# A low part made by an adding DMA instead of VectorE, for every second weight tile of the S5 input projection

## The chip, the cores and the metric

One core of a Trainium2 chip runs the whole kernel. The metric is the device time of one execution in microseconds (us). Before the change it was run three times: 1904.86, 1898.52 and 1904.84 us, a median of 1904.84 us. One further execution was profiled. Engines are named as the profile names them: PE is TensorE's matmul side and PEld its weight loads, DVE is VectorE, ACT is ScalarE, POOL is GpSimd, SP is SyncE, which here only issues DMAs.

## The reference, cut to what matters

The network has two layers over 256 frames of width 2048, a gated linear attention layer and an S5 layer, each with an inner width of 4096. The change lies in the first product of the S5 layer:

```python
proj = u_in @ w_in                 # (256, 2048) @ (2048, 8192), float32
u, z = jnp.split(proj, 2, axis=-1)
...                                # u drives the recurrence, z becomes silu(z)
```

## The kernel before

All weights are float32 and come from HBM in tiles of 128 partitions x 1024 (two blocks of 128 rows by 512 columns, 512 KB). To multiply in the faster fp32r format without losing accuracy, each weight is written as a sum of two fp32r numbers: `hi`, the weight rounded by ScalarE (line 109), and `lo`, the weight minus `hi`, made by VectorE (line 110). The activations are split in the same way, and a product takes three matmuls: hi x hi (line 155), hi x lo of the activation (line 156) and lo of the weight x hi (line 157). The helper `split` makes the two parts, `wload` issues the load on SP's queue, and `st_step` the 24 matmuls of a tile.

The S5 input projection runs in two loops of 64 tiles each: `su` (the half that becomes u, line 1020) and `sz` (the half that becomes z, line 1099). Each is 8 column groups `g` of 8 tiles `kp`. Between the tiles, other work of the layer is worked off: in `su` the preparation of the S5 kernels (`b_pow`, `b_tr`, `s_mm`, `k_out`; the last writes a block `ks` to the DRAM tensor `dk` by a DMA on POOL's queue, line 986) and the recurrence (`scan`); in `sz` the rest of the recurrence and, for each of 32 blocks `f`, `cload` and `mload` (DMAs `cl<-rec` and `mt<-dk` on SP's queue), `cunit` (VectorE products `wc` from `cl`, lines 912 and 913), `xstage` (a VectorE transpose `xT`, line 1066, then a TensorE transpose `psxs`, line 1069) and `ystage` (matmuls `psy`, and a gelu). After `sz` the product with the gate weights (`gl`) begins.

What sets the order: each engine works through its own instructions strictly in the order that a scheduler fixed when the program was built, and waits at each for semaphores. Buffers rotate: `hi` and `lo` have three buffers each, the loaded weight tile `w` has four in this stage, `cl` and `mt` two each. So ScalarE's rounding of tile n+3 must wait until TensorE has done with tile n, and the load of tile n+4 until both readers of tile n's `w` are done (after the change the planned reuse of these four buffers is at a few places three or five tiles on).

Of the kernel before, what the change touches and what calls it, by code (L numbers as in the profile page):

```python
# [8 lines left out]
F32 = mybir.dt.float32  # L9
F32R = mybir.dt.float32r  # L10
AF = mybir.ActivationFunctionType
ALU = mybir.AluOpType
# [3 lines left out]
P = 128  # L16
D = 2048
E = 4096
# [15 lines left out]
def trunk(ctx, tc, x, c, ln_g, ln_b, ada_w, ada_b, gla_w_in, gla_gate_w2, gla_gate_b, gla_norm_g,  # L34
# [3 lines left out]
    V, S, PE = nc.vector, nc.scalar, nc.tensor  # L38
    dma = nc.sync.dma_start
    wdma = nc.gpsimd.dma_start  # L40

    def pool(name, bufs=1, **kw):
        return ctx.enter_context(tc.tile_pool(name=name, bufs=bufs, **kw))
# [3 lines left out]
    hp = pool("whi", 3)  # L47
    lp = pool("wlo", 3)
# [26 lines left out]
    def psm(name):  # L75
        return mm.tile([P, 512], F32, tag="mm", name=name)
# [19 lines left out]
    def pump(rate=1.0):  # L96
        pace[0] += rate
        while pace[0] >= 1.0:
            pace[0] -= 1.0
            if bg:  # L100
                bg.pop(0)()


    last_lo = [None]

    def split(w, name):
        hi = hp.tile([P, 1024], F32R, tag="hi", name="hi" + name)
        lo = lp.tile([P, 1024], F32R, tag="lo", name="lo" + name)
        S.copy(hi, w)  # L109
        last_lo[0] = V.tensor_tensor(lo, w, hi.bitcast(F32), op=ALU.subtract).ins  # L110
        return hi.rearrange("p (k c) -> p k c", k=2), lo.rearrange("p (k c) -> p k c", k=2)
# [15 lines left out]
    def wload(src, k0, c0, name):  # L127
        ring.append(ring.pop(0))
        w = ring[-1]("w" + name)
        dma(w.rearrange("p (k c) -> p k c", k=2),  # L130
            src[k0 * P:(k0 + 2) * P, c0:c0 + 512].rearrange("(k p) c -> p k c", p=P))
        return w
# [13 lines left out]
    def st_step(banks, u, w, kp, last, first=0):  # L146

        hi, lo = w
        for f in range(4):
            for kk in range(2):  # L150
                k = 2 * kp + kk
                wh = hi[:, kk, f * P:(f + 1) * P]
                wl = lo[:, kk, f * P:(f + 1) * P]
                o = banks[f][:, :T]
                PE.matmul(o, lhsT=wh, rhs=u.hi(k), start=(k == first), stop=False)  # L155
                PE.matmul(o, lhsT=wh, rhs=u.lo(k), start=False, stop=False)  # L156
                PE.matmul(o, lhsT=wl, rhs=u.hi(k), start=False, stop=(k == last))  # L157
# [621 lines left out]
    for g in range(8):  # L779
# [3 lines left out]
        for kp in range(8):  # L783
            for _ in range(-(-len(hq) // (8 * (2 - g % 2) - kp))):
                hq.pop(0)()
            w = split(wload(win, 2 * kp, 6144 + g * 512, f"z{g}{kp}"), f"z{g}{kp}")
# [101 lines left out]
    sw = s5_w_in[0]  # L888
# [53 lines left out]
    def s_in(f, ps):  # L942
        v = tp.tile([P, 2, 16, 8], F32, tag="vv", name=f"vv{f}", bufs=2)
        V.transpose(v.rearrange("p b i s -> p s b i"), ps[:, :T].rearrange("p (s b i) -> p s b i", s=8, b=2)[:, ::-1])
        pu = psx(f"psu{f}")
        for b in range(2):
            PE.transpose(pu[:, b * P:(b + 1) * P], v[:, b].rearrange("p i s -> p (i s)"), ident)
        U = Ut[f // 8][:, f % 8]
        S.copy(U, pu[:, :T].rearrange("p (b r) -> p b r", b=2))
# [50 lines left out]
    def bstep(n):  # L1000
        for _ in range(n):
            if bq:
                bq.pop(0)()

    def scan(cidx, h):
        X = sx[:, h, cidx].rearrange("p (r k) n -> p r k n", r=2)
        N = sx[:, h, cidx + 1].rearrange("p (r k) n -> p r k n", r=2)
        t1 = tp.tile([P, 2, 2, 32], F32, tag="sc1", name=f"sca{cidx}{h}", bufs=1)
        t2 = tp.tile([P, 2, 2, 32], F32, tag="sc2", name=f"scb{cidx}{h}", bufs=1)
        lr = l8r.rearrange("p (k n) -> p k n", k=2)[:, :, 32 * h:32 * h + 32]  # L1010
        li = l8i.rearrange("p r (k n) -> p r k n", k=2)[:, :, :, 32 * h:32 * h + 32]
        V.tensor_tensor(t1, X, lr.unsqueeze(1).to_broadcast([P, 2, 2, 32]), op=ALU.mult)
        V.tensor_tensor(t2, X[:, ::-1], li, op=ALU.mult)
        V.tensor_tensor(t1, t1, t2, op=ALU.add)
        V.tensor_tensor(N, N, t1, op=ALU.add)

    for g in range(8):
        banks = [psm(f"su{g}{f}") for f in range(4)]
        for kp in range(8):
            w = split(wload(sw, 2 * kp, g * 512, f"su{g}{kp}"), f"su{g}{kp}")  # L1020
            st_step(banks, u1, w, kp, 15)
            if (g, kp) == (1, 0):
                b_pace[0] = -1.0
            b_pace[0] += 1.5 if g else 0.25
            n = max(0, int(b_pace[0]))
            bstep(n)
            b_pace[0] -= n
            pump(SCAN_RATE)
        for i in range(4):
            s_in(4 * g + i, banks[i])  # L1030
        if g == 4:
            bg.extend([lambda cidx=cidx: scan(cidx, 0) for cidx in range(1, 31)])
# [30 lines left out]
    def xstage(f):  # L1063
        xt_ = tp.tile([P, 2, 4, 32], F32, tag="xt", name=f"xT{f}", bufs=1)
        n = 2 * (f % 16)
        V.transpose(xt_, sx[:, f // 16, 0:32, :, n:n + 2].rearrange("p c r b -> p b r c"))
        px = psx(f"psxs{f}")
        for b in range(2):
            PE.transpose(px[:, b * P:(b + 1) * P], xt_[:, b].rearrange("p r l -> p (r l)"), ident)
        xs = tp.tile([P, 2, 128], F32, tag="xs", name=f"xS{f}", bufs=2)  # L1070
        S.copy(xs, px[:, :T].rearrange("p (b r) -> p b r", b=2))
        xss[f] = xs

    def ystage(f):
        xs = xss[f]
        py = psx(f"psy{f}")
        U = Ut[f // 8][:, f % 8]
        for b in range(2):
            o = py[:, b * P:(b + 1) * P]
            for q in range(4):  # L1080
                PE.matmul(o[32 * q:32 * q + 32], lhsT=U[:, b, 32 * q:32 * q + 32], rhs=mt[f][:, :, 2 * q + b, :], start=True, stop=False)
            for w in wc[f]:
                for q in range(4):
                    PE.matmul(o[32 * q:32 * q + 32], lhsT=xs[:, b, 32 * q:32 * q + 32],
                              rhs=w[:, 2 * q + b].rearrange("p n i -> p (n i)"), start=False, stop=(w is wc[f][-1]))
        yt = tp.tile([P, 8, 32], F32, tag="yt", name=f"yt{f}", bufs=2)
        V.transpose(yt, py[:, :T].rearrange("p (b t i) -> p t b i", b=2, t=8))
        S.activation(U, yt.rearrange("p t c -> p (t c)").rearrange("p (b r) -> p b r", b=2), AF.Gelu_apprx_tanh)

    def cside(f):  # L1090
        cload(f)
        mload(f)
        cunit(f)

    zs = [s8t(f"zs{i}", [8, T]) for i in range(4)]
    for g in range(8):
        banks = [psm(f"sz{g}{f}") for f in range(4)]
        for kp in range(8):
            w = split(wload(sw, 2 * kp, E + g * 512, f"sz{g}{kp}"), f"sz{g}{kp}")
            st_step(banks, u1, w, kp, 15)  # L1100
            if g == 0:
                bstep(1 + kp % 2)
            pump(SCAN_RATE if g == 0 else Y_RATE)
        for f in range(4):
            i = (g * 4 + f) % 8
            S.activation(zs[g // 2][:, i, :], banks[f][:, :T], AF.Silu)  # L1106
        if g == 0:
            bstep(len(bq))
            while bg:
                bg.pop(0)()  # L1110
            tp.close()
            tp.open("tmp2")
            sc1 = [lambda cidx=cidx: scan(cidx, 1) for cidx in range(1, 31)]
            for f in range(34):
                for _ in range(3):
                    if sc1:
                        bg.append(sc1.pop(0))
                if f < 32:
                    bg.append(lambda f=f: cside(f))
                if 1 <= f < 33:  # L1120
                    bg.append(lambda f=f: xstage(f - 1))
                if f >= 2:
                    bg.append(lambda f=f: ystage(f - 2))
# [18 lines left out]
    for g in range(8):  # L1142
        banks = [psm(f"gl{g}{f}") for f in range(4)]
        for kp in range(16):
            w = split(wload(s5_w_glu[0], 2 * kp, g * 512, f"gl{g}{kp}"), f"gl{g}{kp}")
# [121 lines left out]
```

## Time and profile before

| what | value |
|---|---|
| runs | median 1904.84 us (1898.52 to 1904.86) |
| the profiled execution, own time | 1901.91 us |
| its span, first to last instruction | 1900.0 us, granted TensorE clock 0.987 |
| `su`: first to last matmul with `lo` | 783.4 to 1057.9 us, 64 tiles |
| `sz`: the same | 1058.3 to 1330.1 us, 64 tiles |
| matmuls of line 155 in `su` / in `sz` | 512 / 512 |

A row of a group view gives the line of the kernel, the engine, the operation, output and inputs by the program's names, how often, the busy time in us and the mean of one in ns, then the engine's idle time just before these instructions and what ended it. Matmuls are pipelined: one of 0.28 us starts every 0.12 us. A row of a view of waits gives who waited for whom, the total in us, how often, and the longest. A row of a windows view gives a stretch of the span, the busy us of each engine, the granted clock, the mean busy share of the 16 DMA engines and the rate they moved. A row of a timeline gives start, duration, engine, line and operation, and in brackets the engine's idle time before it and what ended that.

### The profile page before, as it was taken

How to read it: one execution, taken by the hardware profiler on the slowest of the kernel's cores; microseconds unless marked ns; L12 is line 12 of the kernel's file. 1: busy time of each engine (PE TensorE's matmuls, PEld its weight loads, DVE VectorE, ACT ScalarE, POOL GpSimd, SP SyncE). 2: the span in 40 equal slices, each digit the busy share in tenths (PEclk: the TensorE clock that was granted, in tenths of full speed). 3: DMA queues.
4: the chain of work that ended last, by engine and by line, in shares of the span. 5: the costliest groups of instructions: out<-in, count | busy, mean ns of one | idle time of the engine just before them, and what ended most of it. 6: DMA issues, size and time to landing. Idle time of an engine off the chain costs nothing.

```text
span 1900.0 us, 35655 instructions
## 1 busy us (share of the span) xinstructions
PE 1833.9 (97%) x14479; PEld 1649.2 (87%) x14479; DVE 1431.4 (75%) x1992; ACT 890.8 (47%) x1229; POOL 27.0 (1%) x44
## 2 busy tenths in 40 slices
PE   7999999999999999899999989999999999999997
PEld 3787797799999888789899889888999999998886
DVE  2788676889899887687799789988577674457555
ACT  3533365655555333654454445445444444444332
POOL 0000000000000000000000000000000000000000
PEclk9999999999999999899999999999999999999998
DMA  9878975789889997555555577897688886558662
GB/s 358 309 254 275 337 245 183 243 281 321 289 286 310 360 339 242 174 153 153 162 143 159 157 207 218 222 244 216 214 270 256 264 265 205 180 184 322 195 194 68
DMA packets 239501, 449.27 MB, mean 236 GB/s; under 512 B 19220, under 2 KB 45262, under 8 KB 238054
## 3 DMA queue, kind: packets, MB, share of 16 engines
q1 hardware_dynamic: 235400, 437.53, 72.3%
q0 software_dynamic: 3168, 8.41, 1.4%
q8 instruction: 114, 1.87, 0.4%
q10 hardware_dynamic: 768, 1.05, 0.2%
q14 instruction: 51, 0.42, 0.1%
HBM read 432.49 MB, written 14.42 MB: 235 GB/s over the span
## 4 chain that ended last, share of the span: by engine, by line
PE 64%; issue 9%; DVE 7%; DMA 5%; ACT 1%; POOL 1%; SPq 0%; DVEq 0%; POOLq 0%; ACTq 0%
PE gl L157 7%; PE gl L155 7%; PE gl L156 6%; PE op L143 6%; PE op L144 6%; PE op L142 6%; PE z L157 3%; PE z L155 3%; PE z L156 3%; DMA cl<-rec 3%; PE su L155 2%; PE su L157 2%; PE su L156 2%; PE sz L155 1%; PE sz L157 1%
## 5 line engine op out<-in xcount | busy, mean ns | idle before, releaser
L155 PE MATMUL gl<-yh,higl 128*128 128x256 f32 x1024 | 291.9, 285 | 3.3 <-ACT higl L109 3.3
L157 PE MATMUL gl<-yh,logl 128*128 128x256 f32 x1024 | 290.1, 284 | 0.0
L156 PE MATMUL gl<-yl,higl 128*128 128x256 f32 x1024 | 290.1, 283 | 0.0
L110 DVE TENSOR_TENSOR logl<-wgl,higl 128x1024 fp32r<-128x1024 f32 x128 | 156.7, 1225 | 139.0 <-ACT higl L109 138.9
L109 ACT CAST higl<-wgl 128x1024 fp32r<-128x1024 f32 x128 | 134.0, 1047 | 202.7 <-PE gl L156 201.0
L155 PEld LDWEIGHTS gl<-yh,higl 128*128 128x128 f32 x1024 | 197.2, 193 | 4.4 <-ACT higl L109 3.5
L156 PEld LDWEIGHTS gl<-yl,higl 128*128 128x128 f32 x1024 | 197.2, 193 | 1.0 <-issue 1.0
L157 PEld LDWEIGHTS gl<-yh,logl 128*128 128x128 f32 x1024 | 197.1, 193 | 0.2 <-DVE logl L110 0.2
L109 ACT CAST hio<-wo 128x1024 fp32r<-128x1024 f32 x105 | 110.7, 1054 | 173.0 <-PE op L144 159.6
L110 DVE TENSOR_TENSOR loo<-wo,hio 128x1024 fp32r<-128x1024 f32 x105 | 128.4, 1224 | 78.3 <-ACT hio L109 77.8
L242 DVE SCALAR_TENSOR_TENSOR acc<-wa,cs,acc 128x512 f32<-128x512 f32 x215 | 160.8, 748 | 4.1 <-DMA wa<-in_ada_w 1.3
L157 PE MATMUL sz<-u1h,losz 128*128 128x256 f32 x512 | 147.1, 288 | 5.2 <-DVE losz L110 5.2
L155 PE MATMUL sz<-u1h,hisz 128*128 128x256 f32 x512 | 150.7, 295 | 0.2 <-ACT zs L1106 0.2
L155 PE MATMUL su<-u1h,hisu 128*128 128x256 f32 x512 | 150.3, 295 | 0.0
L155 PE MATMUL z<-u0h,hiz 128*128 128x256 f32 x512 | 148.7, 290 | 0.5 <-ACT hiz L109 0.5
L156 PE MATMUL su<-u1l,hisu 128*128 128x256 f32 x512 | 147.1, 288 | 0.0
L157 PE MATMUL su<-u1h,losu 128*128 128x256 f32 x512 | 147.0, 288 | 0.0
L157 PE MATMUL z<-u0h,loz 128*128 128x256 f32 x512 | 145.1, 283 | 1.7 <-DVE loz L110 1.7
L156 PE MATMUL sz<-u1l,hisz 128*128 128x256 f32 x512 | 146.1, 285 | 0.0
L156 PE MATMUL z<-u0l,hiz 128*128 128x256 f32 x512 | 144.7, 283 | 0.0
L142 PE MATMUL v<-hiv,u0h 128*128 128x512 f32 x256 | 103.9, 413 | 4.5 <-ACT hiv L109 2.6
L143 PE MATMUL v<-lov,u0h 128*128 128x512 f32 x256 | 103.5, 405 | 4.4 <-DVE lov L110 4.3
(318 smaller groups left out, 4714.5 us busy)
## 6 DMA issues: line engine op xcount, KB each, us to landing
wgl<-in_s_w_glu SPq DMA_DIRECT2D x128, 512.0 KB
wa<-in_ada_w SPq DMA_DIRECT2D x115, 512.0 KB
a<-in_ada_w SPq DMA_DIRECT2D x32, 1024.0 KB
wv<-in_gla_w_in SPq DMA_DIRECT2D x64, 512.0 KB
wz<-in_gla_w_in SPq DMA_DIRECT2D x64, 512.0 KB
wsu<-in_s_w_in SPq DMA_DIRECT2D x64, 512.0 KB
wsz<-in_s_w_in SPq DMA_DIRECT2D x64, 512.0 KB
wo<-in_s_w_out SPq DMA_DIRECT2D x64, 512.0 KB
```

The costliest lines, as they stand in the source:

```text
L109: S.copy(hi, w)
L110: last_lo[0] = V.tensor_tensor(lo, w, hi.bitcast(F32), op=ALU.subtract).ins
L142: PE.matmul(banks[tt], lhsT=uh, rhs=hi[:, kk, :], start=(k == first), stop=False)
L143: PE.matmul(banks[tt], lhsT=uh, rhs=lo[:, kk, :], start=False, stop=False)
L144: PE.matmul(banks[tt], lhsT=ul, rhs=hi[:, kk, :], start=False, stop=(k == last))
L155: PE.matmul(o, lhsT=wh, rhs=u.hi(k), start=(k == first), stop=False)
L156: PE.matmul(o, lhsT=wh, rhs=u.lo(k), start=False, stop=False)
L157: PE.matmul(o, lhsT=wl, rhs=u.hi(k), start=False, stop=(k == last))
L242: V.scalar_tensor_tensor(acc[0], w[:, kk, :], cs[:, k:k + 1], acc[0], op0=ALU.mult, op1=ALU.add)
```

## The change

For odd `kp` in both loops a new helper is used. ScalarE writes `hi` as before, and then writes minus `hi` into `lo`; after that an accumulating DMA on POOL's queue adds the loaded weight tile, SBUF to SBUF, onto `lo`. VectorE's subtraction goes away for these 64 tiles. Even `kp` stays as it was.

```diff
+    def split_dma(w, name):
+
+        hi = hp.tile([P, 1024], F32R, tag="hi", name="hi" + name)
+        lo = lp.tile([P, 1024], F32R, tag="lo", name="lo" + name)
+        S.copy(hi, w)
+        S.mul(lo, hi.bitcast(F32), -1.0)
+        wdma(lo, w, accum_op=ALU.add)
+        return hi.rearrange("p (k c) -> p k c", k=2), lo.rearrange("p (k c) -> p k c", k=2)
...
-            w = split(wload(sw, 2 * kp, g * 512, f"su{g}{kp}"), f"su{g}{kp}")
+            w = (split_dma if kp % 2 else split)(wload(sw, 2 * kp, g * 512, f"su{g}{kp}"), f"su{g}{kp}")
...
-            w = split(wload(sw, 2 * kp, E + g * 512, f"sz{g}{kp}"), f"sz{g}{kp}")
+            w = (split_dma if kp % 2 else split)(wload(sw, 2 * kp, E + g * 512, f"sz{g}{kp}"), f"sz{g}{kp}")
```

All lines below the helper stand nine lower in the changed file (line 986 is 995, 1039 is 1048). In names such as `losu23` the digits are g and kp.

On POOL's queue, in the middle of `su`, before the change only the writes of `ks` stand:

```order
L986 DMA dk_183<-ks3_8400 8x16x128 [waits DMASW1_49,DVE_49]
L986 DMA dk_183<-ks4_8508 8x16x128 [waits DMASW2_49,DVE_49]
L986 DMA dk_183<-ks5_8620 8x16x128 [waits DMASW3_49,DVE_49]
L986 DMA dk_183<-ks6_8728 8x16x128 [waits DMASW4_49,DVE_49]
L986 DMA dk_183<-ks7_8868 8x16x128 [waits DMASW5_49,DVE_49]
```

The same place on POOL's queue after the change:

```order
L112 DMA losu23_8468<-wsu23_8465 128x1024 [waits DMAHW6_49,DMASW4_49,Activation_49]
L995 DMA dk_183<-ks3_8409 8x16x128 [waits DVE_49]
L112 DMA losu25_8577<-wsu25_8574 128x1024 [waits DMAHW3_49,DMASW6_49,Activation_49]
L995 DMA dk_183<-ks4_8518 8x16x128 [waits DMASW5_49,DVE_49]
L112 DMA losu27_8690<-wsu27_8687 128x1024 [waits DMAHW5_49,DMASW0_49,Activation_49]
L995 DMA dk_183<-ks5_8631 8x16x128 [waits DMASW7_49,DVE_49]
```

Each adding DMA now stands between two writes of `ks`, so that it starts only after the write ahead of it, which waits for VectorE, has been issued.

On ScalarE's queue in `su`, the rounding of two tiles before the change:

```order
L109 CAST hisu30_8764<-wsu30_8762 128x1024
L939 COPY wbt8_8604<-pswb80_8605 128x512
L939 COPY wbt8_8604<-pswb81_8611 128x512
L979 COPY ks5_8620<-psk5_8617 128x128
L109 CAST hisu31_8814<-wsu31_8812 128x1024
L969 COPY kT7_8674<-pss7_8656 128x256
```

And two tiles after the change:

```order
L118 CAST hisu24_8526<-wsu24_8524 128x1024
L948 COPY wbt6_8393<-pswb60_8394 128x512
L948 COPY wbt6_8393<-pswb61_8400 128x512
L988 COPY ks3_8409<-psk3_8406 128x128
L110 CAST hisu25_8576<-wsu25_8574 128x1024
L111 ACTIVATE losu25_8577<-hisu25_8576 128x1024
L978 COPY kT5_8463<-pss5_8445 128x256
```

The row of line 111 is new, straight behind the rounding of the odd tile; the copies keep their places among the roundings, and `kT` and all that follows stands one instruction later. An even tile has no second instruction.

On SP's queue early in `sz`, before the change, with what each load waits for:

```order
L130 DMA wsz21_12172<-in_s5_w_in 128x2x512 [waits DMAHW1_49,DVE_49]
L130 DMA wsz22_12214<-in_s5_w_in 128x2x512 [waits DMAHW2_49,DVE_49]
L130 DMA wsz23_12267<-in_s5_w_in 128x2x512 [waits DMAHW4_49,DMAHW3_49,DVE_49]
L1058 DMA mt2_11970<-dk_183 128x1x1024 [waits PE_49]
L130 DMA wsz24_12331<-in_s5_w_in 128x2x512 [waits DMAHW5_49,DMAHW0_49,DVE_49]
L130 DMA wsz25_12373<-in_s5_w_in 128x2x512 [waits DMAHW6_49,DMAHW1_49,DVE_49]
L1039 DMA cl4_12250<-rec_182 128x256 [waits DMAHW7_49,DVE_49]
```

And after the change:

```order
L139 DMA wsz21_12212<-in_s5_w_in 128x2x512 [waits DMAHW1_49,DMASW4_49,Activation_49]
L139 DMA wsz22_12255<-in_s5_w_in 128x2x512 [waits DMAHW2_49,DVE_49]
L1067 DMA mt2_12009<-dk_183 128x1x1024 [waits DMAHW3_49,PE_49]
L139 DMA wsz23_12308<-in_s5_w_in 128x2x512 [waits DMAHW4_49,DMAHW0_49,DVE_49]
L1048 DMA cl4_12291<-rec_182 128x256 [waits DMAHW5_49,DVE_49]
L1050 DMA cl4_12291<-rec_182 64x128 [waits DMAHW6_49]
L139 DMA wsz24_12373<-in_s5_w_in 128x2x512 [waits DMASW5_49]
```

A load that takes over the buffer of an odd tile (here those of tiles 21 and 24) now waits for the semaphore of a POOL DMA (DMASW) where it waited for VectorE (DVE), and the loads of `mt` and `cl` stand one to two places earlier among the weight loads.

## Prediction

> **What bounds the kernel now.** I read the page first, then windows over the two loops, then the waits inside them.
>
> ```profile
> PE 1833.9 (97%) x14479; PEld 1649.2 (87%) x14479; DVE 1431.4 (75%) x1992; ACT 890.8 (47%) x1229; POOL 27.0 (1%) x44
> ```
> ```profile
> 880.00:920.00 40.00, 39.34 (x405) 35.77 (x405) 32.20 (x42) 20.10 (x38) 2.39 (x4) 1.00 0.56 163
> 1000.00:1040.00 40.00, 39.71 (x428) 35.59 (x426) 39.87 (x95) 19.16 (x35) 2.98 (x5) 1.00 0.54 154
> 1160.00:1200.00 40.00, 39.52 (x465) 37.52 (x464) 39.17 (x77) 18.77 (x28) 0.00 (x0) 1.00 0.88 238
> 1240.00:1280.00 40.00, 36.28 (x474) 33.78 (x474) 35.52 (x39) 18.41 (x28) 0.00 (x0) 0.96 0.92 238
> ```
>
> The columns are PE, PEld, DVE, ACT and POOL, then the clock, the DMA share and GB/s. TensorE is the bound. In `su` (the first two rows) it is busy for over 39 of 40 us even where VectorE is full (39.87), so relieving VectorE has nothing to give there. In `sz` VectorE is nearly full and TensorE loses a few us per 40; that is all that can be won. The DMA engines are at 0.54 to 0.56 in `su`, but at 0.88 and 0.92 in `sz`. The waits within `sz`:
>
> ```profile
> PE psxs L1069 <- DVE xT L1066: 9.4, 3, 3.7
> DVE wc L913 <- DMA cl<-rec: 9.1, 6, 2.5
> ACT hisz L109 <- DMA wsz<-in_s_w_in: 13.6, 3, 7.1
> PE sz L157 <- DVE losz L110: 5.2, 2, 5.0
> ```
>
> TensorE waited directly for the subtraction only twice, 5.2 us. Its 9.4 us for `xT` are VectorE's too, but VectorE itself had been waiting for the `cl` loads (9.1 us): the more so as the DMAs are slow.
>
> **What is removed and added.**
>
> ```profile
> L110 DVE TENSOR_TENSOR losu<-wsu,hisu 128x1024 fp32r<-128x1024 f32 x64 | 77.5, 1211 | 12.4 <-ACT hisu L109 12.0
> L109 ACT CAST hisu<-wsu 128x1024 fp32r<-128x1024 f32 x64 | 67.2, 1050 | 77.3 <-issue 36.8 <-PE su L156 34.3 <-PE op L144 5.0
> ```
>
> 64 subtractions of 1.21 us leave VectorE, 77 us in all. ScalarE gets 64 more instructions over the same 128x1024; I price one at its cast, 1.05 us, 67 us in all. ScalarE is busy 20 of 40 us and stays under two thirds; in `su` it idles after most casts (the timeline below), so I cost this at nothing. Without that cover, each would delay the copies behind it by 1.05 us. The adding DMA is the unknown, as no DMA of before adds or goes from SBUF to SBUF. The nearest rows are POOL's own DMAs, from issue to landing: 64 KB of `ks` (first pair) and 1 MB into `rec` (second pair).
>
> ```profile
> L986 POOL DMA_DIRECT2D dk<-ks x32: 597/597/630, 832.6 to 1098.1; - x32
> DMA to landing us min/median/max: 2.0/3.5/4.4
> ...
> L516 POOL DMA_DIRECT2D rec<-lc x2: 1175/1252/1328, 260.3 to 265.1; - x2
> DMA to landing us min/median/max: 6.8/8.0/10.9
> ```
>
> 512 KB on the straight line between the medians is 3.5 + 4.5 x 448/960 = 5.6 us. An adding DMA must also fetch the bytes it adds onto, which makes it 1 MB read and 512 KB written, so 8.0 would be the full doubling. I take **6.3 us**, nearer to the lower since start and writing do not double. The ends are 2.0 and 10.9 us.
>
> In the Trainium skill, "Collectives: The Full Stack", section "The bandwidth ceiling: the fold count and why AG ≠ RS ≠ AR", an add inside a DMA costs no time of its own, but its two source reads share one read queue and halve the rate. No run here shows that yet; by it the landing is nearer to 8.0 us and the sum below comes to about 1954 us, as an estimate (half of 1.7 us on 28 tiles of `su` most of all).
>
> **When must it land?** With three buffers, the cast of a tile starts as TensorE ends the tile three before. TensorE then needs this tile's `lo` after two tiles, that is, about when the cast two places on starts. From this interval the cast and the new instruction go off, 2.1 us; the rest is the DMA's. ScalarE's timeline in the middle of `su`, at the start of `su`, and at two places of `sz`:
>
> ```profile
> 896.17 1.05 ACT L109 CAST hisu<-wsu 128x1024 fp32r<-128x1024 f32 x1 [1.57 <-PE su L156]
> ...
> 900.65 1.06 ACT L109 CAST hisu<-wsu 128x1024 fp32r<-128x1024 f32 x1 [1.62 <-issue]
> ...
> 904.58 1.05 ACT L109 CAST hisu<-wsu 128x1024 fp32r<-128x1024 f32 x1 [1.69 <-PE su L156]
> ```
> ```profile
> 796.18 1.05 ACT L109 CAST hisu<-wsu 128x1024 fp32r<-128x1024 f32 x1
> ...
> 801.02 1.05 ACT L109 CAST hisu<-wsu 128x1024 fp32r<-128x1024 f32 x1 [1.31 <-PE su L156]
> ...
> 806.78 1.05 ACT L109 CAST hisu<-wsu 128x1024 fp32r<-128x1024 f32 x1 [1.46 <-PE su L156]
> ```
> ```profile
> 1090.34 1.05 ACT L109 CAST hisz<-wsz 128x1024 fp32r<-128x1024 f32 x1 [1.94 <-PE sz L156]
> ...
> 1093.59 1.21 ACT L1106 ACTIVATE zs<-sz 128x256 f32<-128x256 f32 x4
> 1094.66 1.07 ACT L109 CAST hisz<-wsz 128x1024 fp32r<-128x1024 f32 x1
> ...
> 1097.42 1.05 ACT L109 CAST hisz<-wsz 128x1024 fp32r<-128x1024 f32 x1
> ...
> 1102.28 1.05 ACT L109 CAST hisz<-wsz 128x1024 fp32r<-128x1024 f32 x1 [1.83 <-PE sz L156]
> ```
> ```profile
> 1128.23 1.03 ACT L109 CAST hisz<-wsz 128x1024 fp32r<-128x1024 f32 x1
> ...
> 1135.81 1.05 ACT L109 CAST hisz<-wsz 128x1024 fp32r<-128x1024 f32 x1 [1.12 <-DMA cl<-rec]
> ```
>
> Middle of `su`: 8.41 - 2.1 = 6.3 us. The DMA just fits: **0**. A stall would count half, since a stall of one odd tile lies inside the interval of the next.
>
> Start of `su` (tiles 5 and 7, counted from its first cast), while tiles still follow closely: 4.84 - 2.1 = 2.7 us for tile 5, so 3.6 us late; tile 7 has 5.76 - 2.1 = 3.7, which the stall of tile 5 lengthens past 6.3. **+3.6**.
>
> Second column group of `sz`: the cast behind the four `zs` copies waits for the end of the first group, so it is the third tile (kp 2) and those at 1090.34, 1097.42 and 1102.28 are odd. The first has 7.1 - 2.1 = 5.0 and is 1.3 late; the next 4.9 - 2.1 + 1.3 = 4.1, 2.2 late. **+3.5**. The third was one of the two that waited for VectorE, 5.0 us; landing 2.1 + 6.3 us after its cast, it waits about half as long: **-2.7**.
>
> From 1120 to 1190:
>
> ```profile
> 1120.00:1160.00 40.00, 23.67 (x85) 16.07 (x84) 12.09 (x10) 1.00 0.74 217
> 1160.00:1190.00 30.00, 20.04 (x71) 13.39 (x70) 12.21 (x10) 1.00 0.82 229
> 1190.00:1330.00 140.00, 68.49 (x240) 46.34 (x240) 33.26 (x28) 0.98 0.87 228
> ```
>
> These rows count the matmuls on `losz` alone, eight to a tile: 156 in the first two, so some 10 odd tiles. Each has 7.58 - 2.1 = 5.5, is 0.8 late, and counts half: **+4**.
>
> The rest of `sz` (third row) has fewer matmuls per us, so the landing fits. But its DMAs are at 0.87 with 228 GB/s. If that share is real work, full is 228/0.87 = 262 GB/s. 240 matmuls are 30 tiles, 15 of them odd; 15 adding DMAs of 0.5 to 1 MB bring 56 to 112 GB/s more, 284 to 340. Over 262 that would stretch 140 us by 12 to 42 us. Against it, the page shows 360 GB/s in a slice of another stage:
>
> ```profile
> GB/s 358 309 254 275 337 245 183 243 281 321 289 286 310 360 339 242 174 153 153 162 143 159 157 207 218 222 244 216 214 270 256 264 265 205 180 184 322 195 194 68
> ```
>
> At that rate nothing would stretch. I take **+12**, the lower of the two stretches and also 2 us on each of the six `cl` waits above; bounds 0 and 42. Late weight buffers go into it: an odd tile's buffer comes free only with the landing, SP waits for that in order, and the loads of `cl` and `mt` stand behind it; the 13.6 us above show that weight loads are late at times already.
>
> VectorE's relief: the 9.4 us for `xT` partly go, since a subtraction or two stands ahead of them, though the `cl` load ends last: **-5**, bounds 0 and -9.4.
>
> On POOL, an adding DMA stands behind a write of `ks`. Two of these in the middle of `su`:
>
> ```profile
> 895.21 0.60 POOL L986 DMA_DIRECT2D dk<-ks  x1 [8.40 <-DVE ks L983]
> 904.45 0.60 POOL L986 DMA_DIRECT2D dk<-ks  x1 [8.65 <-DVE ks L983]
> ```
>
> The one at 895.21 is past before the cast at 896.17 and its second instruction end (898.3): 0. If VectorE made `ks` 3 us later, POOL would hold up the adding DMA.
>
> The sum: 3.6 + 3.5 - 2.7 + 4 + 12 - 5 = +15.4. The profiled execution took 1901.91 us itself (span 1900.0), 2.9 below the median of the runs, so **1917 us**, 0.6% above the median.
>
> **The rivals.** (1) *Everything lands in time*, and the queues swallow the rest. For it: 5.6 us on the straight line, 360 GB/s elsewhere. Then no stall is added, and VectorE's relief stands: -5.2 for the two waits and up to -9.4, so 1887 to 1902. This is the case that ends on the other side; it decides at 2.7 us at the few close tiles and 5.5 us elsewhere in `sz`. (2) *The adding DMA is far slower*, at the 10.9 us end: (10.9 - 6.3)/2 for 28 tiles of `su` is +64, (10.9 - 5.5)/2 for 32 of `sz` +86, with the 12 above some 2060 us. Against it: 10.9 was 1 MB written to DRAM. (3) *The DMA engines become the bound* of the last 140 us: +42 in place of +12, 1947 us. (4) *VectorE's relief changes nothing*, being no bound, and the new costs are as small: within 0.5% of the median.
>
> A rule that speaks against the change: the Trainium skill, "SBUF — State Buffer", section "Who interferes with whom", says that POOL's building of descriptors is held up while VectorE works in a mode with two ports. In this trace the 32 issues above took 597 to 630 ns beside a full VectorE, so nothing of it shows.
>
> **How the numbers follow.** A measurement tells about 0.5% from no change, 1895 to 1914 us. The forecast with rival 3 (1914 to 1965): 0.40. Rival 4 and the upper part of rival 1 (1895 to 1914): 0.33. The lower part of rival 1 (1885 to 1895): 0.17. Rival 2: 0.10. So slower 0.50, same 0.33, faster 0.17. The range 1888 to 1965 leaves out rival 2 and the lowest part of rival 1, some 0.17.
>
> **What would show it.** The landing of the adding DMAs: about 6 us right, under 5 rival 1, over 9 rival 2. TensorE's waits for a DMA into `lo`: a few us early in `su`, most in `sz` before 1190. The DMA share after 1190: near 1.00 for the forecast and rival 3, and longer waits for `cl`. VectorE's busy time should fall by 77 us, ScalarE's rise by 67. The prediction is wrong if TensorE never waits for `lo`, or if it waits all through `su`.

## The result, and the profile after

The changed kernel takes 1970.4 us (1968.72 to 1971.91, 4 runs) against 1904.31 us (1898.52 to 1904.86): a ratio of 1.035, 95% interval 1.0331 to 1.0369. The profiled execution took 1968.72 us, its span is 1967.0 us. The prediction was 1917 us, slower as it came out, but its range ended at 1965.

First the page: busy time of the engines, then the POOL queue's packets, MB and share of the time of the 16 DMA engines (1.4% before).

```profile
PE 1859.2 (95%) x14479; PEld 1669.4 (85%) x14479; DVE 1375.4 (70%) x1928; ACT 956.6 (49%) x1293; POOL 83.9 (4%) x108
...
q0 software_dynamic: 12384, 41.97, 10.4%
```

VectorE has 64 instructions less and 56 us of busy time less, not the 77 us forecast: the 1.21 us of a row overlap its neighbours at both ends (897.38 + 1.21 is past the next start, 898.51, and the one before it ran to 897.54). ScalarE has 64 more and 66 us more. The same four stretches as before, in the windows view of the changed kernel (the two of `sz` lie some 20 us earlier in its work, as `su` ends later):

```profile
880.00:920.00 40.00, 38.06 (x395) 34.10 (x388) 26.47 (x34) 22.26 (x38) 6.17 (x9) 1.00 0.79 214
1000.00:1040.00 40.00, 37.80 (x401) 33.77 (x398) 36.38 (x89) 23.91 (x40) 6.66 (x9) 1.00 0.76 205
1160.00:1200.00 40.00, 32.21 (x336) 30.39 (x335) 29.34 (x65) 18.39 (x25) 3.37 (x4) 0.87 0.89 227
1240.00:1280.00 40.00, 31.78 (x376) 29.68 (x378) 24.52 (x28) 19.62 (x29) 2.92 (x4) 0.87 0.96 238
```

The next to last column is the DMA share. In `su` it rose from about 0.55 to 0.78 and TensorE, full before, now loses about 2 us in 40. In `sz` it stands at 0.89 and 0.96, and TensorE loses 8. The same view over each whole loop, from its first to its last matmul, first of the kernel before, then of the changed one:

```profile
782.10:1058.20 276.10, 273.16 (x2798) 249.44 (x2797) 235.69 (x401) 142.13 (x263) 15.58 (x26) 0.99 0.55 160
1058.00:1330.40 272.40, 255.89 (x3118) 239.29 (x3116) 237.55 (x359) 131.82 (x207) 3.58 (x6) 0.98 0.78 212
```
```profile
782.40:1078.00 295.60, 278.69 (x2798) 252.93 (x2797) 208.63 (x369) 174.98 (x295) 44.89 (x58) 0.98 0.78 207
1077.80:1396.80 319.00, 275.50 (x3118) 256.07 (x3116) 211.70 (x331) 164.96 (x241) 30.23 (x37) 0.92 0.91 232
```

The second column is the length: `su` grew from 276.1 to 295.6 us, `sz` from 272.4 to 319.0. That is the whole loss, 66 us; the rest of the kernel after `sz` takes 570 us in both. Length times share is the time of the DMA engines: 152 us before and 231 after in `su`, 212 and 290 in `sz`, 78 to 79 us more in each.

The loss in `sz` has two parts. Length minus the busy time of PE grew from 16.5 to 43.5 us, and the same 3118 matmuls were busy for 19.6 us longer (275.50 against 255.89). The clock column fits the second part: 0.02 of 272.4 us and 0.08 of 319.0 us are 5 and 26 us of full-speed time. Over the runs below, the clock of a loop tends to be lower where TensorE stood idle longer: in `su` 0.99 with 2.9 us idle (before), 0.98 with 16.9 (after), 0.94 with 27.8 (e6), 0.86 with 96 (e3). So some 20 of the 46.6 us seem to come on top of the waits. No run holds the clock fixed, so it is not shown that the waits lower it. The other engines did not slow down: a cast took 1.05 us and a `wc` product 1.22 us (medians) in both kernels.

By column group (last `lo` matmul of a group to that of the next, us):

| groups | before | after | difference |
|---|---|---|---|
| `su` 1 | 27.7 | 34.7 | +7.0 |
| `su` 2 to 8 | 246.8 | 259.4 | +12.6 |
| `sz` 1 | 35.0 | 34.4 | -0.6 |
| `sz` 2 | 31.8 | 37.3 | +5.5 |
| `sz` 3 and 4 | 57.5 | 73.6 | +16.1 |
| `sz` 5 to 8 | 147.5 | 173.2 | +25.7 |

The two parts of `sz` differ. The windows of groups 2 to 4 and of groups 5 to 8, before and after:

```profile
1093.20:1182.60 89.40, 83.99 (x900) 80.72 (x899) 80.70 (x163) 41.88 (x60) 1.12 (x2) 0.98 0.75 212
1182.60:1330.10 147.50, 137.46 (x1859) 127.68 (x1857) 133.55 (x165) 72.67 (x118) 0.00 (x0) 0.98 0.86 228
```
```profile
1112.40:1223.30 110.90, 92.06 (x900) 87.56 (x899) 77.30 (x171) 53.68 (x72) 10.87 (x13) 0.91 0.89 230
1223.30:1396.50 173.20, 148.61 (x1858) 137.52 (x1857) 116.29 (x132) 90.84 (x138) 13.46 (x16) 0.91 0.96 240
```

In groups 5 to 8 the DMA engines work for 166 us (0.96 of 173.2), more than the 147.5 us that these groups took before.

The changed kernel's view of the tile `losu`, then of `losz`: the new ScalarE instruction, POOL's issue, and the landing (the first three figures of an instruction's row are ns, least, median, most).

```profile
L111 ACT ACTIVATE losu<-hisu x32: 1057/1058/1087, 772.3 to 1064.9; 128x1024 fp32r<-128x1024 f32 x32
L112 POOL DMA_DIRECT2D losu<-wsu x32: 828/865/917, 773.6 to 1066.2; - x32
...
  PE su L166: 5.6, 4
...
DMA to landing us min/median/max: 4.5/5.9/8.4
```
```profile
  PE sz L166: 40.2, 16
...
DMA to landing us min/median/max: 4.5/6.6/10.8
```

So the adding DMA landed as fast as assumed (6.3 us), and in `su` TensorE waited for a low part only 5.6 us in all, in `sz` 40.2. The waits of the changed kernel in `sz` that answer to those shown of before:

```profile
PE sz L166 <- DMA losz<-wsz: 40.2, 16, 5.2
...
DVE wc L922 <- DMA cl<-rec: 15.6, 8, 4.3
...
DVE wc L921 <- DMA cl<-rec: 6.5, 3, 4.8
```

Read alone, this says that `sz` lost 40 us to late low parts (18.8 in groups 2 to 4, 21.5 in groups 5 to 8) and `su` some 14 us to something else. The experiments bear that out for groups 2 to 4 in the main. In groups 5 to 8 that wait is where the loss shows, not what makes it.

### The profile page after: what moved, and what is told of

It is laid out like the page before. It is cut to its first block, busy times and chain, and to the rows that moved or that the text cites. A ratio compares the mean times of both kernels' runs of the same rounds, so it can differ in the third digit from the quotient of the medians.

```text
span 1967.0 us, 35864 instructions
## 1 busy us (share of the span) xinstructions
PE 1859.2 (95%) x14479; PEld 1669.4 (85%) x14479; DVE 1375.4 (70%) x1928; ACT 956.6 (49%) x1293; POOL 83.9 (4%) x108
## 3 DMA queue, kind: packets, MB, share of 16 engines
q10 hardware_dynamic: 768, 1.05, 0.2%
## 4 chain that ended last, share of the span: by engine, by line
PE 66%; DMA 10%; DVE 4%; issue 4%; ACT 2%; SPq 1%; DVEq 0%; POOLq 0%; POOL 0%; ACTq 0%
PE gl L164 6%; PE gl L165 6%; PE gl L166 6%; PE op L151 6%; PE op L152 6%; PE op L153 6%; DMA losz<-wsz 4%; PE z L166 3%; PE z L164 3%; PE z L165 3%; PE su L164 2%; DMA rb<-rec 2%; PE su L166 2%; PE su L165 2%; PE sz L166 2%
## 5 line engine op out<-in xcount | busy, mean ns | idle before, releaser
L118 ACT CAST hio<-wo 128x1024 fp32r<-128x1024 f32 x105 | 110.9, 1056 | 172.9 <-PE op L153 158.5
L166 PE MATMUL sz<-u1h,losz 128*128 128x256 f32 x512 | 155.7, 307 | 40.4 <-DMA losz<-wsz 40.2
L164 PE MATMUL sz<-u1h,hisz 128*128 128x256 f32 x512 | 157.8, 309 | 0.0
L165 PE MATMUL sz<-u1l,hisz 128*128 128x256 f32 x512 | 153.1, 300 | 0.0
L166 PEld LDWEIGHTS sz<-u1h,losz 128*128 128x128 f32 x512 | 107.0, 210 | 45.0 <-DMA losz<-wsz 43.8
L164 PEld LDWEIGHTS sz<-u1h,hisz 128*128 128x128 f32 x512 | 106.5, 208 | 6.7 <-issue 6.0
```

## The experiments

Landing theory: TensorE loses the time by waiting for low parts that come too late for three buffers. Load theory: the adding DMAs take time of the 16 DMA engines, other loads land later, and TensorE loses it whether or not it waits for a low part. In the diffs below, `-` and `+` are against the changed kernel unless it is said otherwise; line numbers shift by a few where lines were added. Lengths of `su` and `sz` are from the first to the last matmul of the loop. The kernel before was run beside each set; its medians were 1902.7 to 1904.3 us, and the ratios go by these. Lengths come from one profiled execution of each run; where two runs have the same code in a loop, their lengths there differ by 3.6 us at most (`sz` of after and e1).

| run | what | time, us | ratio to before, 95% | `su` | `sz` |
|---|---|---|---|---|---|
| before | | 1904.3 | | 276.0 | 272.4 |
| after | | 1970.4 | 1.0331 to 1.0369 | 295.6 | 319.0 |
| e1 | only `sz` changed | 1954.7 | 1.0248 to 1.0301 | 276.3 | 322.6 |
| e2 | only `su` changed | 1924.5 | 1.0088 to 1.0120 | 295.6 | 271.8 |
| e3 | chained dummies | 2023.4 | 1.0606 to 1.0647 | 400.6 | 271.7 |
| e4 | no low part on odd tiles | 1902.3 | 0.9976 to 1.0001 | 276.4 | 273.8 |
| e5 | 48 dummies from `lo` | 1959.0 | 1.0281 to 1.0314 | 310.5 | 293.2 |
| e6 | four buffers | 1979.3 | 1.0375 to 1.0429 | 314.8 | 312.7 |
| e7 | ScalarE's part alone | 1902.1 | 0.9979 to 1.0004 | 275.6 | 272.2 |
| e8 | plain copy | 1944.8 | 1.0204 to 1.0241 | 284.3 | 302.4 |
| e9 | half of `rb` and `mt` | 1938.6 | 1.0167 to 1.0197 | 284.2 | 302.2 |
| e10 | e9's control, from before | 1886.2 | 0.9892 to 0.9921 | 273.6 | 259.8 |
| e11 | half of the adding DMAs | 1944.8 | 1.0173 to 1.0227 | 285.2 | 305.3 |
| e12 | e9 with four buffers | 1929.9 | 1.0099 to 1.0167 | 282.4 | 292.0 |
| e13 | e6 with six weight buffers | 1975.3 | 1.0335 to 1.0431 | 304.4 | 307.8 |
| e14 | e13 with half of `rb` and `mt` | 1935.1 | 1.0127 to 1.0193 | 279.7 | 288.6 |
| e15 | 64 dummies onto `w` | 1982.7 | 1.0369 to 1.0451 | 314.8 | 312.2 |
| e16 | e12 and half of `cl` | 1916.3 | 1.0055 to 1.0099 | 284.8 | 278.2 |
| e17 | e9 and half of `cl` | 1930.0 | 1.0112 to 1.0166 | 283.2 | 296.9 |
| e18 | e16's and e17's control | 1886.4 | 0.9896 to 0.9934 | 274.0 | 259.0 |

### Each loop by itself (e1, e2)

```diff
-            w = (split_dma if kp % 2 else split)(wload(sw, 2 * kp, g * 512, f"su{g}{kp}"), f"su{g}{kp}")
+            w = split(wload(sw, 2 * kp, g * 512, f"su{g}{kp}"), f"su{g}{kp}")
```

This is e1; e2 has the same edit in the `sz` loop.

> The su loop splits all tiles on VectorE as in the kernel before; only the sz loop uses the adding DMA. After minus before, by the last matmul of each loop, was +20 us in su and +46 us in sz. If each loop pays for its own adding DMAs: su ends as before at about 1058, sz takes about 319 us, the run about 1904 + 46 = 1950. Rival: part of sz's loss is handed on by su (work of su that runs late into sz): then sz takes clearly less, 295 to 305 us, and the run is 1927 to 1937.

> Only the su loop uses the adding DMA. If each loop pays for its own: su ends at about 1078, sz takes 272 us as before, the run about 1924. Rival (work pushed from su into sz costs there): sz takes 285 us or more, the run 1937 or more.

e1 costs 50 us and e2 20 us. Each loop pays for its own adding DMAs (322.6 and 295.6 us), and the other one is as before. So the two can be studied apart.

### What VectorE's relief is worth, and what ScalarE's part costs (e4, e7)

```diff
-        lo = lp.tile([P, 1024], F32R, tag="lo", name="lo" + name)
         S.copy(hi, w)
-        S.mul(lo, hi.bitcast(F32), -1.0)
-        wdma(lo, w, accum_op=ALU.add)
...
+        return hi.rearrange("p (k c) -> p k c", k=2), hi.rearrange("p (k c) -> p k c", k=2)
```

That was e4. In e7 VectorE subtracts, and ScalarE's instruction writes where nobody reads:

```diff
-        S.mul(lo, hi.bitcast(F32), -1.0)
-        wdma(lo, w, accum_op=ALU.add)
+        V.tensor_tensor(lo, w, hi.bitcast(F32), op=ALU.subtract)
+        if name < "sz6":
+            S.mul(zs[3].rearrange("p k t -> p (k t)")[:, 0:1024], hi.bitcast(F32), -1.0)
```

> Odd tiles of su and sz make no low part at all: the cast alone, and the third matmul of each trio takes the high part again, so the odd tiles' low part of the weights is left out of the result. It shows what taking 64 subtractions (77 us) from VectorE can give with nothing in their place. The prediction's term was -5 us (0 to -9.4): 1895 to 1904. Rival: VectorE's queue did hold TensorE up in more places than its waits show, and the relief gives 15 us or more, below 1890.

> VectorE subtracts for all tiles as before and no adding DMA is issued; ScalarE alone also writes minus the high part of odd tiles into a stretch that nobody reads (56 of the 64). Prediction and landing theory: ScalarE's instruction is hidden, 1904 to 1908. Rival (its place ahead of ScalarE's copies for the state work delays TensorE): su +10 or more, the run 1915 or more.

e4 bounds what any way of taking these subtractions from VectorE can give: nothing that its runs can tell from zero, 0.24% at most. `sz` without them, in the windows view of e4:

```profile
1058.80:1332.60 273.80, 257.99 (x3118) 241.08 (x3116) 209.41 (x331) 130.20 (x208) 3.56 (x6) 0.98 0.78 208
```

VectorE has 28 us less to do than before (209.41 against 237.55), and the loop is no shorter. e7 costs nothing either: the 56 instructions that ScalarE makes here are hidden. What is left of the change is the DMA.

### Load without a wait for the low part (e3, e5, e15)

In all three VectorE makes the low parts again, and an adding 512 KB DMA runs beside it for which TensorE does not wait. In e3 all dummies add onto one stretch of SBUF:

```diff
-        S.mul(lo, hi.bitcast(F32), -1.0)
-        wdma(lo, w, accum_op=ALU.add)
+        V.tensor_tensor(lo, w, hi.bitcast(F32), op=ALU.subtract)
+        if name < "sz6":
+            wdma(zs[3].rearrange("p k t -> p (k t)")[:, 0:1024], u1.his[0].rearrange("p k t -> p (k t)")[:, 0:1024].bitcast(F32), accum_op=ALU.add)
```

> VectorE subtracts for every tile as before, and ScalarE's extra instruction is gone. Beside it each odd tile of su, and of sz up to its sixth column group, issues an adding 512 KB DMA between two stretches of SBUF that no matmul waits for (56 of 64). The output is the reference's. Landing theory (TensorE loses the time by waiting for low parts that land late): no such wait is left, so 1904 to 1910. Load theory (the adding DMAs' time on the 16 DMA engines makes the other loads late): most of the loss stays, su +12 to +15 and sz +25 to +40 up to its sixth group, 1940 to 1955, with TensorE waiting for weights rather than for low parts.

This run answers another question than the one asked. The view of waits of e3 over the whole span:

```profile
POOL zs L113 <- DMA zs<-u1h: 271.3, 55, 8.1
...
ACT ks L989 <- DMA dk<-ks: 113.4, 18, 17.0
```

With one target, each dummy waits for the one before, the `ks` writes stand behind them in POOL's queue, and ScalarE waits for its single `ks` buffer. That costs `su` 125 us and says nothing about load. All 56 dummies are issued by 1122.6 us, while `su` still runs, so `sz` had none, and its 271.7 us speak neither way. e5 copies from the finished low part to four targets in turn; e15 adds onto the tile's own weight buffer, once both readers are done with it:

```diff
+        if name < "sz4":
+            n = int(name[2]) * 4 + int(name[3]) // 2
+            z = zs[2 + n % 2][:, 2 * (n % 4 - n % 2):2 * (n % 4 - n % 2) + 4]
+            wdma(z.rearrange("p k t -> p (k t)"), lo.bitcast(F32), accum_op=ALU.add)
```
```diff
+        wdma(w, u1.his[0].rearrange("p k t -> p (k t)")[:, 0:1024].bitcast(F32), accum_op=ALU.add)
```

> The run with the chained dummies confounded load with a new wait (each dummy waited for the one before, and the ks writes stood behind them). Here the low parts come from VectorE again, and each odd tile of su, and of sz up to its fourth column group (48 in all), issues an adding 512 KB DMA from its finished low part into one of four stretches of SBUF that nobody reads. So it starts as in the changed kernel, moves as much, and nobody waits for it. Landing theory (a low part comes too late for three high and three low buffers): the sz groups 2 to 4, 28.6 to 31.8 us before and 36 to 38 us after, are back below 31 us each, su loses under 5 us, the run 1904 to 1912. Load theory: these groups stay at 35 us or more, su +12, the run 1935 to 1945.

> VectorE makes all low parts. Each odd tile also issues an adding 512 KB DMA whose target is its own weight buffer, after both readers are done, so that the buffer is held until it has landed; 64 of them, nobody waits for a low part. Held-buffer theory: worse than the dummies that held no weight buffer (su 310, sz 293 with 16 of them): sz 315 us or more. Two-limit theory: the load alone, sz 290 to 312.

e5 costs 56 us. With the full 64 in e15 it is 80 us (78 by the ratio), more than the change itself, though all low parts come from VectorE. So a loss of this size needs no wait for low parts. But it lies elsewhere: groups 2 to 4 of `sz`, 89.4 us before and 110.9 after, take 97.6 us in e5 and 98.2 in e15, so there the load alone costs 8 to 9 of the 21.5 us. In e5 they take 36.0, 28.6 and 33.0 us, between the two theories. Groups 5 to 8 of e15 take 179.4 us, 6 more than in the changed kernel. e15's `sz`, 312.2 us, falls just between its two forecasts. Where e15's time goes in `sz`, from its view of waits:

```profile
ACT hisz L110 <- DMA wsz<-in_s_w_in: 24.6, 11, 3.7
ACT hisz L118 <- DMA wsz<-in_s_w_in: 19.8, 8, 4.4
DVE wc L922 <- DMA cl<-rec: 17.8, 10, 5.1
PE psy L1090 <- DMA mt<-dk: 16.7, 7, 5.4
```

Every other load is late: the weights (13.6 us of waiting before), `cl` (9.1 on that line before) and `mt`. That `su` takes 311 to 315 us here and 296 in the changed kernel has a candidate: there VectorE has 28 to 31 us less to do, and can catch up after a late load. This was not tried by itself, and e6 below speaks against it: 315 us with the same relief. e15 holds the weight buffer until the landing, as the changed kernel does, and e5 holds the `lo` buffer, so neither is load quite alone.

### Half the packet time, and half the number (e8, e11)

```diff
-        wdma(lo, w, accum_op=ALU.add)
+        wdma(lo, w)
```
```diff
-            w = (split_dma if kp % 2 else split)(wload(
+            w = (split_dma if kp % 4 == 3 else split)(wload(
```

The second edit, e11, stands in both loops.

> As the changed kernel, but the DMA copies the weight tile into the low part instead of adding it, so the low part of odd tiles is the tile itself. An adding 4 KB packet took 328 ns and a plain one of POOL's 159 ns, so the 64 DMAs take half of the engines' time and land earlier, by an estimate from that at 4 to 5 us instead of 6 to 6.6. Landing theory: the bound of a tile in sz falls from 4.6 to about 3.7 us, groups 2 to 4 take 30 to 32 us, the run 1915 to 1935. Load theory: half of the loss goes, 1935 to 1940, spread over both loops.

> Only every fourth weight tile (32 of 128) gets its low part by the adding DMA, the others by VectorE. The DMA time added to sz is 43 us in place of 85. Load theory: su +5 to +10, sz +12 to +23, the run 1922 to 1937. Landing theory: the next odd cast is eight tiles' buffers away and the landing of 6 us is hidden, 1904 to 1912.

By the records of single packets, one of 4 KB took 328 ns (median) where it adds, and 174 to 176 ns in `su` of e8 where it copies. Times 128, over 16 engines, that is 2.6 and 1.4 us for a tile. e8's view of the tile `losu`:

```profile
L112 POOL DMA_DIRECT2D losu<-wsu x32: 528/547/566, 771.6 to 1054.0; - x32
...
DMA to landing us min/median/max: 2.9/3.9/7.4
```

The Trainium skill, "Collectives: The Full Stack", section "The bandwidth ceiling: the fold count and why AG ≠ RS ≠ AR", says of a collective's reduce step that the add is free but its two reads halve the rate; the packets agree (328 against 175 ns).

In `su` the loss grows with the DMA time that was added, length times share minus the 152 us of before: 36 us (e11) cost 9.2, 41 us (e8) cost 8.3, 79 us (after) cost 19.6. That is no price for each microsecond of DMA time: the first group, where TensorE waits for low parts, lost 5.8, 5.9 and 7.0 of it, and groups 2 to 8 lost 3.5, 2.4 and 12.6. In `sz` 35 us cost 33, 57 cost 30, 78 cost 47. Both runs came out slower than either theory had said: e8 at 1944.8 us against 1940 at most, e11 at 1944.8 against 1937. e11's expectation of the landing theory was wrong in itself: three `hi` buffers leave a tile two tiles of time however many tiles use the DMA, and in `sz` of e11 TensorE still waited 23.9 us for ten low parts.

### Through which loads: rb in su (e9, e10)

```diff
-            bload(f // 2)
+            rb[f // 2] = rb[f // 2 - 1] if f % 4 == 2 else bload(f // 2) or rb[f // 2]
...
-        mload(f)
+        mt[f] = mt[f - 1] if f % 2 else mload(f) or mt[f]
```

e10 is the same edit to the kernel before.

> As the changed kernel with all 64 adding DMAs, but half of two other loads are left out: every second rb load (8 of 16, in su) and every second mt load (16 of 32, in sz); the state work then uses the tile loaded before, so its result is not the reference's. A 512 KB mt load takes about 128 x 250 ns / 16 = 2.0 us of all 16 DMA engines, so sz needs about 290 - 32 = 258 us of DMA time in place of 290 (0.91 of 319). Load theory: at the same 0.91 that is 284 us, so sz falls from 319 to 278 to 295 us and su from 294 to 274 to 284, the run to 1920 to 1940. Landing theory (three buffers, low part too late): the waits for low parts stay near 40 us, sz stays at 310 us or more, the run at 1950 or more.

> The control: the same loads left out of the kernel before. Its DMA engines were busy 0.54 of su and 0.78 of sz, so both theories expect little: su 270 to 274 us, sz 262 to 272 us, the run 1888 to 1905. If it gains 20 us or more, the lighter kernel's gain says nothing on the adding DMAs.

`rb` has two buffers. SP loads the next one when TensorE is done with the last (`pss`), and VectorE's first reader of it is `pt`. The timeline in the middle of `su` before, SP's row and VectorE's:

```profile
898.30 0.37 SPq L899 DMA_DIRECT2D rb<-rec  x1
...
902.88 1.08 DVE L929 TENSOR_TENSOR pt<-rb 128x896 f32<-128x896 f32 x1
```

The timeline after, with VectorE's next transpose and the matmuls of TensorE that wait for it:

```profile
907.16 0.37 SPq L908 DMA_DIRECT2D rb<-rec  x1
...
915.22 1.09 DVE L938 TENSOR_TENSOR pt<-rb 128x896 f32<-128x896 f32 x1 [3.23 <-DMA rb<-rec]
...
916.43 0.59 DVE L968 STREAM_TRANSPOSE sx<-pss 128x256 f32<-128x256 f32 x1
...
917.08 0.64 PE L975 MATMUL pss<-wb,rb 128*32 128x128 f32 x16 [1.62 <-DVE sx L968]
```

By the packets, the first load landed 3.9 us after its issue, 0.7 us before it was needed; the second 7.5 us after. Over the 16 loads the median went from 4.2 to 6.2 us. VectorE then idles 3.23 us, does `sx` late behind it, and TensorE, whose queue has `pss` next, stands for 1.62 us. The waits of before hardly name this load, as it came in just in time. In the waits of `su`, `DVE pt` behind `rb` grew from 2.8 us (5 times) to 17.2 (10 times), and TensorE's `pss` behind `sx` from 0.4 to 11.0.

With half of these loads gone, TensorE has no wait for `sx` from 820 us on, and groups 2 to 8 of e9's `su` take 245.2 us, against 245.0 in the control, e10, and 259.4 in the changed kernel: the 12.6 us are explained, with all 32 adding DMAs still there and a DMA share of 0.76. The first group is not cured (37.4 against 27.1 us): there TensorE still waits 6.6 us for low parts.

`sz` did not follow: it lost 42.4 us over its control (302.2 against 259.8; the control, with fewer loads, had itself become shorter by 12.6), hardly less than the 46.6 of the change, at a DMA share of 0.84. It lies between what the two theories had said (295 at most, 310 at least).

### Buffers, and what holds sz (e6, e12, e13, e14)

```diff
-        hi = hp.tile([P, 1024], F32R, tag="hi", name="hi" + name)
-        lo = lp.tile([P, 1024], F32R, tag="lo", name="lo" + name)
+        if name[3] in "37" and name < "sz6":
+            hi, lo = (zs[3][:, i:i + 4].rearrange("p k t -> p (k t)") for i in (0, 4))
+        else:
+            hi = hp.tile([P, 1024], F32R, tag="hi", name="hi" + name)
+            lo = lp.tile([P, 1024], F32R, tag="lo", name="lo" + name)
...
+    zs = [s8t(f"zs{i}", [8, T], F32R if i == 3 else F32) for i in range(4)]
```

This is e6; the last of the four `zs` tiles is thereby rounded to fp32r. e13 adds two weight buffers:

```diff
+    spare6 = [lambda name, i=i: zs[2][:, i:i + 4].rearrange("p k t -> p (k t)") for i in (0, 4)]
+    ring_add(spare6)
...
+            if (g, kp) == (4, 0):
+                [ring_drop(b) for b in spare6]
```

e12 and e14 are e6 and e13 with e9's loads left out.

> As the changed kernel, but every fourth tile of su, and of sz up to its sixth column group, takes its high and low part in 8 KB that the zs rows need only later, so four high and four low buffers take turns there and three in the last two groups. Three high buffers bound a pair of tiles: the cast of an odd tile starts when the tile three before it is done, and cast, negation, issue and landing (1.1 + 1.1 + 0.8 + 6) must fit into the two tiles between, so a tile takes at least 4.5 us. Landing theory: with one more buffer there are three tiles between, the bound falls to 3 us, the sz groups 2 to 4 return to 29 to 32 us each, the run to 1925 to 1945. Load theory: with the DMA engines at 0.9 and more they stay at 35 us or more and the run at 1960 to 1970.

> Four high and low buffers (up to the sixth sz group) and half of the rb and mt loads left out, so the result is not the reference's. Two-limit theory (landing on three buffers, and DMA time, each near 313 us): both are relaxed, sz 265 to 285 us (260 in the control without adding DMAs), su 274 to 284. Held-buffer theory (the weight buffer kept until the landing, SP's queue in order behind it): neither touches that, sz stays at 295 us or more.

> Four high and low buffers and six weight buffers instead of four (the two more up to the fourth sz group), all loads made. Held-buffer theory: SP no longer stands before weight buffers, su falls from 315 to 285 or less and sz from 313 to 295 or less. Two-limit theory: the DMA engines' time is as before, su stays above 295 and sz at 305 to 318.

> All three relaxed: four high and low buffers, six weight buffers, half of the rb and mt loads left out (not the reference's result). Both theories: sz 262 to 280 us, su 274 to 282. If sz stays at 295 us or more, the loss has a cause that neither names.

e6, the waits in `sz`:

```profile
DVE wc L925 <- DMA cl<-rec: 21.5, 10, 4.3
ACT hisz L113 <- DMA wsz<-in_s_w_in: 18.9, 7, 5.7
...
DVE wc L924 <- DMA cl<-rec: 16.2, 7, 4.1
...
PE psy L1094 <- DMA mt<-dk: 12.3, 4, 4.8
...
ACT zs L113 <- DMA wsz<-in_s_w_in: 9.5, 3, 5.1
ACT hisz L121 <- DMA wsz<-in_s_w_in: 9.2, 4, 3.8
```

TensorE's waits for low parts fell from 40 to 14 us, and the loop from 319 only to 313. Groups 2 to 4 became 12 us shorter (31.8, 36.4 and 30.4 us, between the two forecasts), and groups 5 to 8 became 6 us longer. The waits moved to `cl` (37.7 us on the two lines, 22.1 in the changed kernel), to the weights (37.6 against 6.7) and to `mt` (12.3 against 1.2). That `su` became longer by 19 us with more buffers was not expected. It goes through `rb` again, as with half of those loads gone groups 2 to 8 of `su` fall from 278.6 us (e6) to 245.9 (e12); why four buffers make these loads worse stays open. Six weight buffers (e13) seem to help by 10 us in `su` and 5 in `sz`, but `su` starts 11 us later in e13 and e14 than in e6 (793 against 782 us). The whole run gains 4 us, and e14 is 5 us slower than e12. That is far from what the held-buffer theory asked. e12 lost 32.2 us in `sz` over the control, e14 28.8, against 42.4 with three buffers. Both lengths, 292.0 and 288.6 us, lie between the forecasts, so no theory had the whole of it.

### The last load of sz (e16, e17, e18)

```diff
-        cload(f)
+        cl[f] = cl[f - 1] if f % 2 else cload(f) or cl[f]
```

This is added to e12 (e16), to e9 (e17) and to e10 (e18).

> As the run with four high and low buffers and half of the rb and mt loads left out, and half of the cl loads left out too (not the reference's result). Refill theory (the cl tile is loaded only when its reader is done, and lands 1 to 2 us later under the load, as rb in su): sz falls from 292 to within 12 us of its control, 262 to 274 us. DMA-time theory: the cl loads left out are small (16 x 192 KB, some 10 us of the DMA engines), so sz stays at 282 us or more.

> The same loads left out with three high and low buffers. Refill theory, with the landing of low parts still awaited: sz 280 to 295 us, the waits for low parts 25 to 40 us. If the waits for low parts were the larger part, sz stays at 298 us or more.

> The control: the kernel before with half of the rb, mt and cl loads left out. sz 255 to 262 us, su 272 to 275, the run 1880 to 1890. If sz falls below 250, the comparison with the other two goes by the difference alone.

e16's `sz` is 278.2 us, 19.2 over its control; with the landing awaited on three buffers (e17) it is 37.9 over. From e17's view of waits in `sz`, the one that remained for TensorE:

```profile
PE sz L166 <- DMA losz<-wsz: 30.7, 15, 5.7
```

The steps over the controls, with the half loads: 42.4 us; with four buffers 32.2; with half of `cl` as well 19.2; half of `cl` alone 37.9 (e17's profiled execution was its slowest, 6.5 us over the median of its runs). By column group, `sz` in us:

| groups | control e10 | e9 | e12, four buffers | e17, half of `cl` | e16, both | control e18 |
|---|---|---|---|---|---|---|
| 2 to 4 | 87.8 | 108.0 | 93.0 | 108.7 | 93.9 | 86.9 |
| 5 to 8 | 137.6 | 159.5 | 164.3 | 153.4 | 149.5 | 137.7 |

In groups 2 to 4 the fourth buffer takes off 15 us of about 20, with or without the `cl` loads, and the `cl` loads change nothing. So there the landing on three buffers makes most of the loss. In groups 5 to 8 the buffer gives nothing by itself (it is there for group 5 and 6 only), and half of `cl` takes off 6 us alone and 15 with it. The limits of `sz` follow each other in time. That the weights and `mt` stand close behind is argued from the waits and was not tried apart. e16's 278.2 us lies between the refill theory (274 at most) and the DMA-time theory (282 at least). Of its last 19 us, TensorE's waits for low parts make some 12; the rest stays open.

## Why the prediction was wrong, step by step

- **The landing, 6.3 us**: right. Medians were 5.9 and 6.6 us; the greatest, 10.8, came in `sz` under load.
- **ScalarE at nothing**: right (e7, 0.9979 to 1.0004). **VectorE's relief, -5**: nothing that e4 can tell from zero, the upper end of its bounds. Its busy time fell by 56 us, not 77.
- **Middle of `su`, 0**: the step that was reasoned, that the landing just fits, held: 5.6 us of waits in all of `su`. Yet groups 2 to 8 lost 12.6 us, through `rb`. This is the step that failed: the sum had no term for it, as it asked only who waits for the adding DMA, not whose load it delays.
- **Start of `su`, +3.6**: +7.0. Most of TensorE's 5.6 us before low parts fell on tiles 3, 5 and 7; the place was right.
- **Second group of `sz`, +0.8 in sum, and 1120 to 1190, +4**: groups 2 to 4 lost 21.5 us. The mechanism was right and the term too small: TensorE waited 18.8 us for low parts there, where the working had 3.5 + 4. A fourth buffer takes off 12 us with all loads made (e6) and 15 with half of `rb` and `mt` (e9 to e12), and 8 to 9 us are load alone (e5, e15). The intervals were worked out with 6.3 us for each landing, one interval of 7.58 us stood for ten tiles, and they came from the kernel before, where other loads were in time.
- **The rest of `sz`, +12, bounds 0 and 42**: +25.7 in groups 5 to 8, within the bounds. The load was seen here, and only here, because the share was 0.87; the row of `su`, at 0.55, was taken for free. The sign that was named, a share near 1.00, came (0.96 over these groups), and so did longer waits for `cl`. Waits for low parts, put "most in `sz` before 1190", were as long here (21.5 us), where the landing was said to fit.

So what failed is the price of the load outside the last 140 us: nothing was put down for it in `su` and in groups 2 to 4 of `sz`. What the runs showed in its place is 2.6 us of all 16 DMA engines for each adding DMA, some 79 us in each loop. At a share of 0.78 the `rb` loads, which had 0.7 us to spare in the place shown, already pay 12.6 us for it. Beside it the landing in groups 2 to 4 and the stretch of groups 5 to 8 were each taken too small. How much of these 25.7 us is the DMA engines' time, late `cl` loads or the lower clock is not shown apart. Rival 3 (the DMA engines become the bound) had the mechanism of groups 5 to 8, but left out `su` and the first half of `sz`. The rule on the halved rate, cited ahead, gave some 1954 us, nearer than the sum, though by the wrong way: it was spent on the landing in `su`, where TensorE hardly waited, and the landing came out at 5.9 and 6.6 us, not 8.0. That nearness is luck. Rival 1 fell as low parts did come late and e4 found no relief to be had. Rival 4 was right that the relief changes nothing, and wrong on the new costs.

No version that computes the whole result beats the kernel before, and e4 says why: the work that the change removes costs nothing where it is.

## What to carry to other kernels

Before work is moved to a DMA, count its time on the DMA engines, packets times packet time over 16, and look for loads into two buffers that land just ahead of their first reader: here such loads paid at a share of 0.78, long before it neared 1. And ask first what the relief is worth, by leaving the work out: here one run without the subtractions would have ended the matter. When buffers are added against a late transfer and the loop stays as long, look at which other wait grew, and compare the loop part by part: here the buffer did help in one part, and another limit held the next.

## What the hardware showed that was not expected

- POOL issued an adding 512 KB DMA in 0.865 us and the same copy without the add in 0.547 us; the 4 KB packets took 328 and about 175 ns.
- At a DMA share of 0.78, with over a fifth of the engines' time idle on the mean, the loads of `rb` took 6.2 us from issue to landing in place of 4.2 at 0.55.
- The granted clock in `sz` fell from 0.98 to 0.92 in the mean, and the same matmuls took 19.6 us longer. Which part of the loss that is by itself was not tried apart.
